# Expert biases of a top-4 mixture of experts: 64x64 tiled fp32 matmuls replaced by fp32r matmuls over the whole 128x128 array

## The chip, the core and the metric

One core of one Trainium2 chip runs the whole program. The metric is the device time of one execution in microseconds (us); the figure for a kernel is the median of its runs. Instructions run on five engines, each with its own queue in program order: PE (TensorE, matmuls; its weight loads are shown apart as PEld), DVE (VectorE), ACT (ScalarE), POOL (GpSimd) and SP (SyncE, which here issues the transfers of weights).

## The reference

A decoder block on 512 tokens of width 1024: a mixer (a state-space branch and a pooling branch), and then a mixture of 32 experts, of which each token goes to four. The change lies in the experts' biases `b_gu` and `b_down`.

```python
def moe_ffn(h, w_router, b_router, w_gu, b_gu, w_down, b_down):
    logits = xt.astype(f32) @ w_router.astype(f32) + b_router.astype(f32)
    top_val, top_idx = lax.top_k(logits, TOP_K)
    gate = jax.nn.softmax(top_val, axis=-1)
    ...
    def expert_block(args):
        xblk, e = args
        gu = xblk @ w_gu[e] + b_gu[e]              # 1024 -> 2048
        glu, lin = jnp.split(gu, 2, axis=-1)
        glu = jnp.minimum(glu, SWIGLU_LIMIT)
        lin = jnp.clip(lin, -SWIGLU_LIMIT, SWIGLU_LIMIT)
        act = glu * jax.nn.sigmoid(SWIGLU_ALPHA * glu) * (lin + 1.0)
        return act @ w_down[e] + b_down[e]         # 1024 -> 1024
    ...
    y = jax.ops.segment_sum(yb.astype(f32) * row_gate[:, None], row_tok, num_segments=T + 1)[:T]
```

## The kernel before

The mixer takes about the first 715 us; the rest is the experts. An expert's weights come as 12 pieces of 1 MB (8 for the up projection, 4 for the down projection), fetched by SP (`fetch`, L765) into a ring of buffers, as far ahead as buffers are free.

The experts are sorted by their number of tokens. An expert with more than 64 tokens is a **full block** of up to 128 rows. Its products run as three fp32r matmuls over the whole array (L1104 to L1106), for which ACT and DVE first split each half piece of weights into a high part `wh` (L113, ACT) and a low part `wl` (L114, DVE). An expert with at most 64 tokens is a **half block**: its products are fp32 matmuls with 128x64 tiles of the array (L1099), two tiles side by side; its weights need no split. A fp32 matmul leaves two records in the trace. The tiles of PSUM, `mm` and `ss`, hold one bank of 512 columns each; a half block has two column tiles in one bank, one on partitions 0 to 63 and one on 64 to 127. 17 blocks are full, 16 are half (one of these is the second block of the largest expert). The order is fixed: one full expert, two half ones, five times a full and a half one, the largest expert (a full and a half block), a half one, again five times a full and a half one, five full ones in a row, two half ones. The loop issues up(u) and then down(u-1); other small work (turning of the next rows, L1060 and L1066; gathers; activations) is hooked between the pieces.

Each bank starts with its biases: `biases` writes them into PSUM by a matmul with `start=True`, and the products add to them. The table of biases `bt` holds the 32 experts' rows as high and low parts on 64 partitions (a half of the 3072 columns on partitions 0 to 63, the other half on 64 to 127); a column with ones in two rows (`E`, from the router's tile `RM`) picks the expert. For a half block that is one 64x64 fp32 matmul per column tile (L1091): four for an up projection, two for a down projection. For a full block it is one 64x128 fp32r matmul per bank (L1093): four and two.

```python
            r, c = (n0 + n) // 3 * 64, (n0 + n) % 3 * 512
            one, rows = sel[r:r + 64, :], bt[r:r + 64, c:c + 512]
            if x.half:
                TE.matmul(rows_of(ps, n), one.bitcast(F32).to_broadcast([64, 64]), rows.bitcast(F32), start=True, stop=False)
            else:
                TE.matmul(ps[n], one.to_broadcast([64, P]), rows, start=True, stop=False)
```

POOL gathers the rows of a block from DRAM (L1046), multiplies a block's result (L1165, after ACT's L1164) and sends it to DRAM by a scatter that adds (L1168). The Tile framework's scheduler decides the order of instructions on each engine.

Of the kernel before, what the change touches and what calls it, by code (L numbers as in the profile page):

```python
# [31 lines left out]
# columns of the constant array  # L32
C_ID, C_TRI, C_IOTA, C_RC, C_P, C_P5, C_B, C_PM, C_NP = 0, 128, 256, 385, 449, 450, 451, 455, 457
C_KR, C_KC, C_BD, C_CAP, C_H = 458, 490, 491, 495, 527
C_N = 528
C_STRI, C_E = 528, 656
C_ALL = 688
# columns of the per-feature array
Q_CW, Q_CB, Q_SN, Q_PS, Q_NM, Q_C, Q_NF, Q_DS, Q_FN, Q_BA = 0, 96, 120, 136, 144, 152, 160, 168, 184, 192
Q_N = 208  # L40
# columns of the row array (one row, the same for every partition)
# [4 lines left out]
# experts in the order of the number of their tokens, after the FIXED first ones: the tokens that a rank has room for  # L46
# [18 lines left out]
def hybrid_block(ctx: ExitStack, tc: tile.TileContext, cst, cols, rows, xt, xf, wad0, wada, bada,  # L65
# [8 lines left out]
    # places that only the mixer needs stand side by side in one tile, which becomes one of the ring's  # L74
    shared = dict(t1=0, t2=512, dt=1024, ac=1152, dte=1280, eac=1408, cdk=1536, cwh=1664)
# [40 lines left out]
    # ---------------------------------------------------------------- constants  # L116
# [8 lines left out]
    ct = T_("q9", C_ALL - C_N)  # L125
    SP.dma_start(ct, cst[:, C_N:C_ALL])
    qc = T_("cols", Q_N)
    SP.dma_start(qc, cols)
# [3 lines left out]
    tri = cs[:, C_TRI:C_TRI + P]  # L132
# [27 lines left out]
    # ------------------------------------------------- activation of the conditioning  # L160
# [6 lines left out]
    # the shift and scale of the features, a quarter at a time; the first weights run between  # L167
# [22 lines left out]
    cwh = T_("cwh", 120)  # L190
    V.tensor_scalar(cwh, qc[:, 0:120], 0.5, None, op0=ALU.mult)
# [3 lines left out]
    # adaLN: groups of 512 outputs side by side, each on a quarter of the array's columns; rows, then columns  # L195
# [14 lines left out]
    # RMS statistic of x, on every partition  # L210
# [21 lines left out]
    # h of two of the eight tiles of features: the rows of the weights by their number mod 4, each on a quarter of its own  # L232
# [22 lines left out]
    # out tile of 128 features by all tokens  # L255
# [43 lines left out]
    def early():  # L299
# [6 lines left out]
        for r in range(4):  # L306
            SP.dma_start(br[r * 32:(r + 1) * 32, :], ball[:, (r // 2) * 1536:(r // 2 + 1) * 1536])
# [4 lines left out]
    # ---------------------------------------------------------------- dt  # L312
# [56 lines left out]
    # the other adaLN rows; the router's weights with the second norm's scale, and its row of constants  # L369
# [43 lines left out]
    # ---------------------------------------------------------------- pooling branch  # L413
# [15 lines left out]
    def pooled(ps, gi):  # L429
# [11 lines left out]
        tt(m[:, 0:win], s[:, 0:win], cs[:, C_RC + gi * 16:C_RC + gi * 16 + win], ALU.mult)  # L441
# [53 lines left out]
    # ---------------------------------------------------------------- SSD branch  # L495
# [78 lines left out]
    # y, features by tokens: a pair of heads side by side, each on its half of the array's columns  # L574
# [87 lines left out]
    # ---------------------------------------------------------------- gates and merge  # L662
# [51 lines left out]
    # ---------------------------------------------------------------- the adaLN rows in use from here on  # L714
# [21 lines left out]
    # weights of an expert that is known, or stands in a register  # L736
# [766 lines left out]
```

## Time and profile before

| | |
|---|---|
| median of 3 runs | 1942.31 us (1941.54 to 1943.63) |
| span of the profiled execution | 1945.2 us, no time of its own is given beside it |
| PE busy | 1867.3 us, 96% |
| PE weight loads | 1174.8 us, 60% |
| DVE busy | 1212.3 us, 62% |
| ACT busy | 947.9 us, 49% |
| POOL busy | 195.5 us, 10% |
| moved by DMA | 527.82 MB, 271 GB/s over the span |

The span runs from the first to the last instruction of one execution that the profiler recorded. Busy times are sums of instructions' times; on PE the end of a matmul overlaps the start of the next, so the distance from start to start says what a matmul costs. Times below are us from the start of the span.

### The profile page before, as it was taken

To read this page: it belongs to the slowest core of one execution; us is meant where nothing else is said; L and a number is where in the kernel's file an instruction comes from. 1 tells how busy PE (TensorE), PEld (TensorE's weight loads), DVE (VectorE), ACT (ScalarE), POOL (GpSimd) and SP (SyncE) were. 2 spreads that over 40 slices of the span, in tenths; PEclk is the share of its full clock that TensorE was granted. 3 is DMA by queue.
4 is the path that set the end of the run, shared out by engine and by line. 5 is a ranking of instruction groups with operands and counts; after the bars stand their busy time and mean duration, and the time that the engine had idled before them with its cause. 6 is when DMAs were issued, how large, how long until landed. Compare 5 with 4: busy or idle time off the path is not lost. (4 is left out here: it accounts for less than half of the span.)

```text
span 1945.2 us, 23545 instructions
## 1 busy us (share of the span) xinstructions
PE 1867.3 (96%) x8496; PEld 1174.8 (60%) x8497; DVE 1212.3 (62%) x1803; ACT 947.9 (49%) x1458; POOL 195.5 (10%) x149
## 2 busy tenths in 40 slices
PE   6999999999999999999999999999999999999995
PEld 3777687768678875545545545355464464677641
DVE  5878676746564568446646645475475474789823
ACT  4433646455452454444545544254454455677722
POOL 0000000010100000211111201022012012111111
PEclk8999999999999999999999999999999999999998
DMA  8265132343552577998999986889999999988894
GB/s 335 91 258 198 66 134 105 130 109 122 111 179 87 195 294 294 390 408 325 368 356 347 372 341 250 343 306 364 345 374 349 352 371 336 376 334 326 309 340 164
DMA packets 102441, 527.82 MB, mean 271 GB/s; under 512 B 11449, under 2 KB 11961, under 8 KB 60080
## 3 DMA queue, kind: packets, MB, share of 16 engines
q1 hardware_dynamic: 90256, 498.14, 66.6%
q0 software_dynamic: 11184, 25.50, 6.2%
q10 hardware_dynamic: 880, 2.64, 0.4%
q8 instruction: 68, 1.11, 0.2%
q14 instruction: 53, 0.43, 0.1%
HBM read 502.89 MB, written 25.77 MB: 272 GB/s over the span
## 5 line engine op out<-in xcount | busy, mean ns | idle before, releaser
L114 DVE TENSOR_TENSOR wl<-r,wh 128x1024 fp32r<-128x1024 f32 x246 | 301.9, 1251 | 125.1 <-ACT wh L113 123.7
L113 ACT ACTIVATE wh<-r 128x1024 fp32r<-128x1024 f32 x246 | 254.0, 1056 | 143.9 <-PE mm L260 56.3
L114 DVE TENSOR_TENSOR wl<-S,wh 128x1024 fp32r<-128x1024 f32 x186 | 228.5, 1262 | 41.5 <-ACT wh L113 41.0
L1105 PE MATMUL mm<-wl,S 128*128 128x512 f32 x540 | 219.4, 406 | 8.0 <-DVE wl L114 7.7
L113 ACT ACTIVATE wh<-S 128x1024 fp32r<-128x1024 f32 x186 | 189.9, 1056 | 63.7 <-PE mm L1106 37.5
L1106 PE MATMUL mm<-wh,S 128*128 128x512 f32 x540 | 216.8, 401 | 0.0
L259 PE MATMUL mm<-S,wh 128*128 128x512 f32 x512 | 207.8, 407 | 3.9 <-ACT S L113 3.9
L261 PE MATMUL mm<-S,wl 128*128 128x512 f32 x512 | 206.6, 404 | 1.5 <-DVE wl L114 1.5
L260 PE MATMUL mm<-S,wh 128*128 128x512 f32 x512 | 206.6, 404 | 0.0
L1104 PE MATMUL mm<-wh,S 128*128 128x512 f32 x540 | 179.8, 406 | 7.8 <-ACT wh L113 7.8
L1140 DVE TENSOR_SCALAR q<-mm 128x512 f32<-128x512 f32 x49 | 33.0, 688 | 162.7 <-PE mm L1099 132.1
L1165 POOL TENSOR_TENSOR y<-y,q 128x512 f32<-128x512 f32 x47 | 63.8, 1369 | 674.5 <-ACT y L1164 674.5
L1104 PEld LDWEIGHTS mm<-wh,S 128*128 128x128 f32 x540 | 101.3, 190 | 50.0 <-ACT wh L113 16.1
L1105 PEld LDWEIGHTS mm<-wl,S 128*128 128x128 f32 x540 | 103.5, 192 | 45.5 <-DVE wl L114 14.0
L1141 ACT ACTIVATE q<-q 128x512 f32<-128x512 f32 x50 | 31.3, 631 | 200.0 <-DVE q L1140 199.8
L259 PEld LDWEIGHTS mm<-S,wh 128*128 128x128 f32 x512 | 97.3, 190 | 32.8 <-issue 7.1
L1106 PEld LDWEIGHTS mm<-wh,S 128*128 128x128 f32 x540 | 103.6, 192 | 22.2
L261 PEld LDWEIGHTS mm<-S,wl 128*128 128x128 f32 x512 | 97.3, 190 | 30.9 <-issue 7.7
L260 PEld LDWEIGHTS mm<-S,wh 128*128 128x128 f32 x512 | 97.2, 190 | 26.8 <-issue 4.2
L1105 PE MATMUL ss<-wl,S 128*128 128x512 f32 x240 | 100.3, 418 | 1.0 <-DVE wl L114 0.8
L1099 PE MATMUL mm<-S,S 128*64 128x512 f32 x408 | 97.5, 597 | 0.0
L1106 PE MATMUL ss<-wh,S 128*128 128x512 f32 x240 | 96.0, 400 | 0.0
(500 smaller groups left out, 3145.7 us busy)
## 6 DMA issues: line engine op xcount, KB each, us to landing
S<-in_wgu SPq DMA_DIRECT2D x113, 1024.0 KB, 8.0
r<-in_wgu SPq DMA_DIRECT2D x97, 1024.0 KB, 8.5
S<-in_wdn SPq DMA_DIRECT2D x61, 1024.0 KB, 8.4
r<-in_wdn SPq DMA_DIRECT2D x44, 1024.0 KB, 10.9
bc<-in_wgu SPq DMA_DIRECT2D x23, 1024.0 KB, 7.5
Z<-in_wgu SPq DMA_DIRECT2D x23, 1024.0 KB, 7.7
r<-in_wada SPq DMA_DIRECT2D x16, 1024.0 KB, 6.1
r<-in_wx SPq DMA_DIRECT2D x12, 1024.0 KB, 6.2
```

Source lines behind the costliest of these rows:

```text
L113: S.activation(hi, src, AF.Copy)
L114: V.tensor_tensor(lo, src, hi.bitcast(F32), op=ALU.subtract)
L259: TE.matmul(ps, a, hh(k), start=k == 0, stop=False)
L260: TE.matmul(ps, a, hl(k), start=False, stop=False)
L261: TE.matmul(ps, b, hh(k), start=False, stop=k == KD - 1)
L1099: TE.matmul(rows_of(ps, n0 + i), x.c[k], hl[:, o + i * 512:o + (i + 1) * 512], start=False, stop=stop)
L1104: TE.matmul(p, x.h[k], h, start=False, stop=False)
L1105: TE.matmul(p, x.h[k], l, start=False, stop=False)
L1106: TE.matmul(p, x.l[k], h, start=False, stop=stop)
L1140: V.tensor_scalar(g, pg, LIM, None, op0=ALU.min)
L1141: S.activation(t, g, AF.Tanh, scale=ALPHA / 2)
L1165: G.tensor_tensor(yn, yn, gaf2[0] if half else gaf[n], op=ALU.mult)
```

## The change

The table of biases is laid out anew on the host: the even tiles of 512 columns stand on partitions 0 to 63, the odd ones on 64 to 127. A half block's two column tiles of a bank then come from one fp32r matmul over the whole array (`p` is the whole bank): the stationary operand `sel["wide"]` is a 128x128 block-diagonal matrix with the expert's column in both blocks (tiles `sw0`, `sw1`). A full block's bias is a matmul of 128 rows whose column `sel["cols"]` is zero in the other half. A new function `select`, called at the first step of the down projection before, makes these operands on POOL: one multiplication of 128x2 per expert, and two copies of 64x64 for a half block. The constants that the kernel reads at its start are split differently (two more transfers; `tri`, `rcnt` and `cwh` come into a tile that the mixer shares). Comments are removed, so line numbers shift: L1091 becomes L1097, L1093 becomes L1100, L1099 becomes L1106, L1104 to L1106 become L1111 to L1113.

```diff
@@ -304,12 +310,12 @@
         for r in range(4):
-            SP.dma_start(br[r * 32:(r + 1) * 32, :], ball[:, (r // 2) * 1536:(r // 2 + 1) * 1536])
+            SP.dma_start(br[r * 32:(r + 1) * 32, :], ball[r // 2])
         S.activation(bt, br, AF.Copy)
...
     def biases(x, ps, sel, n0):
-        for n in range(len(ps) * (2 if x.half else 1)):
-            r, c = (n0 + n) // 3 * 64, (n0 + n) % 3 * 512
-            one, rows = sel[r:r + 64, :], bt[r:r + 64, c:c + 512]
+        for n, p in enumerate(ps):
             if x.half:
-                TE.matmul(rows_of(ps, n), one.bitcast(F32).to_broadcast([64, 64]), rows.bitcast(F32), start=True, stop=False)
+                c = n0 // 2 + n
+                TE.matmul(p, sel["wide"], bt[:, c * 512:(c + 1) * 512], start=True, stop=False)
             else:
-                TE.matmul(ps[n], one.to_broadcast([64, P]), rows, start=True, stop=False)
+                h, c = (n0 + n) % 2, (n0 + n) // 2
+                TE.matmul(p, sel["cols"][:, h:h + 1].to_broadcast([P, P]), bt[:, c * 512:(c + 1) * 512], start=True, stop=False)
...
+    def sel_halves(out_, e):
+        stt(out_, cs[:, C_PM:C_PM + 2], e, cs[:, C_HM:C_HM + 2], ALU.is_equal, ALU.mult)
...
     def sel_of(u):
         if u < FIXED:
-            return sel0[:, 2 * u:2 * u + 1]
-        return rk["RM"][:, order[u]:order[u] + 1]
+            return dict(cols=sel0[:, 2 * u:2 * u + 2])
+        return dict(cols=sels[u % 2], wide=wides[u % 2])
+
+    sels = [T_(f"sel{i + 1}", 2, F32R) for i in range(2)]
+    wides = [T_(f"sw{i}", P, F32R) for i in range(2)]
+    for w in wides:
+        G.memset(w.bitcast(U32), 0)
+
+    def select(u):
+        if u >= NE:
+            return
+        both = sts[u]["half"] or u == big
+        e = rk["RM"][:, order[u]:order[u] + 1].bitcast(F32)
+        G.tensor_tensor(sels[u % 2], cs[:, C_HM:C_HM + 2], e.to_broadcast([P, 2]), op=ALU.mult)
+        for h in range(2 if both else 0):
+            hs = slice(h * 64, (h + 1) * 64)
+            G.tensor_copy(wides[u % 2][hs, hs], e[hs, :].to_broadcast([64, 64]))
...
             hooks[2] = hooks.get(2, []) + [lambda: turned(u + 1)]
+            if u >= FIXED:
+                hooks[0] = hooks.get(0, []) + [lambda: select(u + 1)]
...
+    c[:, C_HM] = i < 64
     c[:, C_H] = i >= 64
...
-        ball=A(np.concatenate([i["b_gu"][0], i["b_down"][0]], axis=1)),
+        ball=A(np.concatenate([i["b_gu"][0], i["b_down"][0]], axis=1).reshape(NE, 3, 2, 512).transpose(2, 0, 1, 3).reshape(2, NE, 1536)),
```

**PE, the up projection of a half block.** This is the place where a down projection of one half block (tile `ss_902`, products from the weights `S0`, `S1`, `S4`) ends and the banks `mm_918` and `mm_919` of the next half block's up projection are begun; in the trace of before it is the stretch from about 986 to 995 us. L1060 (L1066 after) turns rows of the next block over the whole array. Before:

```order
3443 L1060 MATMUL ss_912_6649<-cst_4_70,q10_911_6643 128x128 x4
3444 L1060 MATMUL mm_915_6663<-cst_4_70,S6_716_5259 128x128
3445 L1091 MATMUL mm_918_6697<-bt_63_381,E_698_5159 64x512
3446 L1099 MATMUL ss_902_6611<-S1_913_6656,r3_867_6297 64x512 x4
3447 L1091 MATMUL mm_918_6697<-bt_63_381,E_698_5159 64x512
3448 L1091 MATMUL mm_919_6698<-bt_63_381,E_698_5159 64x512
3449 L1099 MATMUL ss_902_6611<-S4_916_6676,r3_867_6297 64x512 x4
3450 L1091 MATMUL mm_919_6698<-bt_63_381,E_698_5159 64x512
```

After, at the same place:

```order
3443 L1066 MATMUL ss_916_6662<-cst_4_70,q10_915_6656 128x128 x4
3444 L1066 MATMUL mm_919_6676<-cst_4_70,S6_720_5267 128x128
3445 L1097 MATMUL mm_922_6710<-bt_63_383,sw0_695_5147 128x512
3446 L1097 MATMUL mm_923_6711<-bt_63_383,sw0_695_5147 128x512
3447 L1106 MATMUL ss_906_6622<-S1_917_6669,r3_871_6307 64x512 x4
```

Three stretches of 64x64 matmuls (one, two and one of them) have become two matmuls over the whole array, which stand directly behind the turning; the last four products of the down projection (`S4`) now stand further behind, after the small matmuls of the full array that follow (L1038 and others, not shown).

**PE, the down projection of a half block.** Its bank (`ss_968`, after `ss_972`) is begun among the products of a full block; in the trace of before this is at 1018 us, where a second L1091 follows at 1025 us. Before:

```order
3538 L1053 LDWEIGHTS wrt_955_6939
3539 L1053 MATMUL ss_956_6944<-GV_61_375,wrt_955_6939 128x3
3540 L1091 MATMUL ss_968_7094<-bt_63_381,E_698_5159 64x512
3541 L1105 MATMUL ss_934_6781<-wl0_710_5229,S7_901_6610 128x512
3542 L1106 MATMUL ss_934_6781<-wh0_708_5227,S7_901_6610 128x512
```

After:

```order
3537 L1059 LDWEIGHTS wrt_959_6951
3538 L1059 MATMUL ss_960_6956<-GV_61_377,wrt_959_6951 128x3
3539 L1097 MATMUL ss_972_7106<-bt_63_383,sw0_695_5147 128x512
3540 L1112 MATMUL ss_938_6792<-wl0_714_5237,S7_905_6621 128x512
3541 L1113 MATMUL ss_938_6792<-wh0_712_5235,S7_905_6621 128x512
```

The place of the first of the two is kept; the second one is gone.

**POOL, the making of the selectors.** A stretch of POOL's queue after the change, one full and one half expert long, with what each instruction waits for in brackets; L1052 gathers rows, L1172 multiplies a result, L1175 sends it. Before, the same queue holds these three kinds alone.

```order
58 L1052 DMA S6_720_5267<-h_d_4671,idx_1_896_6484 80x1024 [waits DVE_49,PE_49]
59 L1276 CAST sw0_695_5147<-E_702_5167 64x64 [waits PE_49]
60 L1276 CAST sw0_695_5147<-E_702_5167 64x64 [waits DMASW2_49,DMASW3_49,DMASW1_49,Pool_49]
61 L1172 TENSOR_TENSOR y_887_6424<-y_887_6424,q8_580_4361 128x512 [waits Activation_49,Pool_49]
62 L1172 TENSOR_TENSOR y_887_6424<-y_887_6424,q9_581_4362 128x512 [waits Activation_49]
63 L1175 DMA y_d_124<-y_887_6424,idx_3_757_5565 640x1024 [waits Pool_49]
64 L1273 TENSOR_TENSOR sel2_694_5146<-cst_4_70,E_702_5167 128x2 [waits PE_49]
65 L1052 DMA S6_720_5267<-h_d_4671,idx_2_928_6738 128x512 [waits DVE_49]
```

The two copies of a half expert's selector stand between a gather and a multiplication, and the second one waits for gathers and scatters on POOL's DMA queue; the multiplication for a full expert's selector stands behind a scatter.

## Rows read from the trace of the kernel before

**Rows 1.** The page's busy time, share of the span and instructions of each engine.

```profile
PE 1867.3 (96%) x8496; PEld 1174.8 (60%) x8497; DVE 1212.3 (62%) x1803; ACT 947.9 (49%) x1458; POOL 195.5 (10%) x149
```

**Rows 2.** Busy time by stretch (from:to, length, then busy us and instructions of PE, PEld, DVE, ACT, POOL, then granted clock of PE as a share of the full one, busy share of the DMA engines, GB/s): nearly the whole expert phase, and one period of a full and a half expert.

```profile
720.00:1900.00 1180.00, 1146.49 (x5000) 641.90 (x5001) 723.36 (x1001) 606.08 (x851) 170.50 (x115) 0.99 0.92 345
955.90:1028.60 72.70, 70.08 (x308) 38.38 (x307) 42.40 (x57) 36.12 (x52) 10.01 (x7) 1.00 0.94 360
```

**Rows 3.** Waits in the expert phase, from 720 us on: who waited for what, us in total, how often, the longest. SPq is the queue that fetches the weights, L765 its issue.

```profile
SPq L765 <- DVE wl L114: 436.5, 163, 7.9
SPq L765 <- PE ss L1099: 215.9, 62, 5.5
ACT wh L113 <- DMA S<-in_wgu: 13.7, 2, 12.2
```

**Rows 4.** The matmuls that write biases, grouped by line, operands and shape: count, then busy us and mean ns of one, then idle time before them and what ended it.

```profile
L1091 PE MATMUL mm<-bt,E 64*64 64x512 f32 x120 | 43.0, 612 | 0.0
L1091 PE MATMUL ss<-bt,E 64*64 64x512 f32 x72 | 31.9, 627 | 0.0
L1093 PE MATMUL mm<-bt,E 64*128 64x512 f32 x64 | 29.4, 484 | 5.4 <-DVE q L1142 4.5 <-ACT q L1068 0.4 <-ACT b L1068 0.4
L1093 PE MATMUL ss<-bt,E 64*128 64x512 f32 x32 | 12.4, 452 | 0.0
```

**Rows 5.** PE in order of time (start, duration, instruction, how many in the row), where a half block's up projection is begun.

```profile
987.89 0.27 PE L1060 MATMUL mm<-cst,S 128*128 128x128 f32 x1
988.09 1.07 PE L1091 MATMUL mm<-bt,E 64*64 64x512 f32 x2
989.09 1.94 PE L1099 MATMUL ss<-S,r 128*64 128x512 f32 x8
990.96 1.08 PE L1091 MATMUL mm<-bt,E 64*64 64x512 f32 x4
991.97 1.94 PE L1099 MATMUL ss<-r,r 128*64 128x512 f32 x8
993.83 1.07 PE L1091 MATMUL mm<-bt,E 64*64 64x512 f32 x2
994.83 0.18 PE L1032 MATMUL ss<-tokc,a 128*128 128x2 bf16 x1
```

**Rows 6.** The same view, where a half block's down projection is begun among a full block's products.

```profile
1018.22 0.25 PE L1053 MATMUL ss<-GV,wrt 128*128 128x3 bf16 x4
1018.41 1.07 PE L1091 MATMUL ss<-bt,E 64*64 64x512 f32 x2
1019.41 0.50 PE L1105 MATMUL ss<-wl,S 128*128 128x512 f32 x1
1019.74 0.39 PE L1106 MATMUL ss<-wh,S 128*128 128x512 f32 x1
1019.97 0.39 PE L1105 MATMUL ss<-wl,S 128*128 128x512 f32 x1
...
1024.59 0.62 PE L1104 MATMUL ss<-wh,S 128*128 128x512 f32 x2
1025.15 1.07 PE L1091 MATMUL ss<-bt,E 64*64 64x512 f32 x2
1026.14 0.51 PE L1105 MATMUL ss<-wl,S 128*128 128x512 f32 x1
1026.49 0.40 PE L1106 MATMUL ss<-wh,S 128*128 128x512 f32 x1
```

**Rows 7.** The same view, where a full block's up projection is begun among a half block's products, and the end of these; in brackets the idle time before a row and what ended it.

```profile
998.80 0.50 PE L1093 MATMUL mm<-bt,E 64*128 64x512 f32 x1
999.23 1.94 PE L1099 MATMUL mm<-r,S 128*64 128x512 f32 x8
...
1012.02 0.50 PE L1093 MATMUL mm<-bt,E 64*128 64x512 f32 x1
1012.88 0.49 PE L1093 MATMUL mm<-bt,E 64*128 64x512 f32 x1 [0.36 <-DVE q L1142]
1014.21 0.55 PE L1060 MATMUL ss<-cst,q 128*128 128x128 f32 x3 [0.84 <-DVE q L107]
```

**Rows 8.** Busy time by stretch, columns as in rows 2: a full block's up projection, its down projection (in which the next half block's down projection is begun), the next full block's up projection, and a full block's down projection in the row of five full ones.

```profile
955.90:979.50 23.60, 22.17 (x94) 16.87 (x92) 18.74 (x16) 16.05 (x17) 4.68 (x3) 1.00 0.99 382
1012.00:1028.60 16.60, 15.40 (x73) 10.50 (x72) 13.58 (x20) 10.32 (x12) 1.35 (x1) 1.00 1.01 401
1028.60:1053.70 25.10, 23.67 (x93) 18.08 (x91) 18.89 (x16) 16.05 (x17) 4.67 (x3) 0.93 1.00 386
1709.20:1726.50 17.30, 16.96 (x81) 11.70 (x79) 17.30 (x21) 15.10 (x25) 0.00 (x0) 1.00 0.71 262
```

**Rows 9.** POOL in order of time around one gather (first two rows); the transfers from 990 to 1110 us, by kind, with the median us from issue to landing (third row); and PE where the next half block's up projection is begun (last row).

```profile
1017.71 1.35 POOL L1046 DMA_INDIRECT S<-h_d,idx  x1 [17.69 <-issue]
1029.14 2.52 POOL L1165 TENSOR_TENSOR y<-y,q 128x512 f32<-128x512 f32 x2 [10.09 <-ACT y L1164]
S<-h_d,idx POOLq DMA_INDIRECT x4, 6.0
1062.35 1.07 PE L1091 MATMUL mm<-bt,E 64*64 64x512 f32 x2
```

**Rows 10.** What the DMA engines moved from 990 to 1110 us, GB/s in 40 slices of 3 us.

```profile
GB/s 284 355 318 173 324 420 416 429 421 431 414 315 414 419 283 329 347 422 429 431 415 410 117 328 213 281 354 264 249 337 412 429 429 437 426 412 412 422 419 212
```

More of the change, by code (lines that the diff above doesn't have):

```diff
@@ L30 @@
 ALPHA = 1.702
[L33 to L40, printed above, removed]
+C_ID, C_IOTA, C_P, C_P5, C_B, C_PM, C_NP = 0, 128, 257, 258, 259, 263, 265
+C_KR, C_KC, C_BD, C_CAP, C_HM = 266, 298, 299, 303, 335
+C_H, C_N = C_HM + 1, C_HM + 2
+C_TRI, C_RC = C_N, C_N + 128
+C_STRI = C_RC + 64
+C_E = C_STRI + 128
+C_ALL = C_E + 32
+Q_CB, Q_CW = 96, 120
+Q_SN, Q_PS, Q_NM, Q_C, Q_NF, Q_DS, Q_FN, Q_BA = 0, 16, 24, 32, 40, 48, 64, 72
+Q_N = 88
 R_AL, R_DB, R_BR = 0, 32, 64
@@ L72, in hybrid_block @@
     uid = [0]
-    shared = dict(t1=0, t2=512, dt=1024, ac=1152, dte=1280, eac=1408, cdk=1536, cwh=1664)
+    shared = dict(t1=0, t2=512, dt=1024, ac=1152, dte=1280, eac=1408, cdk=1536, cwh=1664, tri=1784)
     Z = sb.tile([P, 2048], F32, tag="Z", name="Z")
@@ L124, in hybrid_block @@
     SP.dma_start(cs, cst[:, 0:C_N])
-    ct = T_("q9", C_ALL - C_N)
-    SP.dma_start(ct, cst[:, C_N:C_ALL])
+    ct = T_("q9", C_ALL - C_STRI)
+    SP.dma_start(ct, cst[:, C_STRI:C_ALL])
     qc = T_("cols", Q_N)
-    SP.dma_start(qc, cols)
+    SP.dma_start(qc, cols[:, Q_CW:Q_CW + Q_N])
+    cwh, trc = T_("cwh", Q_CW), T_("tri", C_STRI - C_TRI)
+    SP.dma_start(cwh, cols[:, 0:Q_CW])
+    SP.dma_start(trc, cst[:, C_TRI:C_STRI])
     rw = T_("rows", R_N)
@@ L131, in hybrid_block @@
     ident = cs[:, C_ID:C_ID + P]
-    tri = cs[:, C_TRI:C_TRI + P]
+    tri, rcnt = trc[:, 0:P], trc[:, P:P + 64]
     iota = cs[:, C_IOTA:C_IOTA + P]
@@ L189, in hybrid_block @@
     V.tensor_tensor(b12[32:64, :], b12r[32:64, :], b12[32:64, :].bitcast(F32), op=ALU.subtract)
-    cwh = T_("cwh", 120)
-    V.tensor_scalar(cwh, qc[:, 0:120], 0.5, None, op0=ALU.mult)
+    V.tensor_scalar(cwh, cwh, 0.5, None, op0=ALU.mult)
     y_d = dr.tile([T + P, D], F32, name="y_d")
@@ L440, in pooled @@
         stt(m[:, win:512], s[:, win:512], 1.0 / win, u[:, win:512], ALU.mult, ALU.subtract)
-        tt(m[:, 0:win], s[:, 0:win], cs[:, C_RC + gi * 16:C_RC + gi * 16 + win], ALU.mult)
+        tt(m[:, 0:win], s[:, 0:win], rcnt[:, gi * 16:gi * 16 + win], ALU.mult)
         tt(m[:, 0:win], m[:, 0:win], u[:, 0:win], ALU.subtract)
@@ L1231, in tabled @@
         eT = T_("eT", 2, F32R)
-        V.tensor_scalar(eT, cs[:, C_PM:C_PM + 2], ec[:, 0:1], None, op0=ALU.is_equal)
-        return dict(pos=lambda b: pu[:, b:b + 1], gv=lambda b: gvu[:, b * 3:(b + 1) * 3], sel=eT[:, 0:1], **weights(ev))
+        sel_halves(eT, ec[:, 0:1])
+        return dict(pos=lambda b: pu[:, b:b + 1], gv=lambda b: gvu[:, b * 3:(b + 1) * 3], sel=dict(cols=eT), **weights(ev))
     def pos_of(u):
@@ L1318, in rows_from_here @@
         xe2.extend([xet[:, 0:D], xet[:, D:2 * D]])
-    extra = {0: {0: [rows_from_here, permute], 1: [lambda: prep(1)], 2: [gates], 3: [permute_gates], 4: [lambda: prep(0)],
+    extra = {0: {0: [rows_from_here, permute], 1: [lambda: prep(1), lambda: select(1)], 2: [gates], 3: [permute_gates], 4: [lambda: prep(0)],
                  6: [first_gates, lambda: prep(2)]},
```

2 lines of the change are left out of this document (1 added, 1 removed).

## The prediction

> **What bounds the kernel now.** I read first the busy times of the page, then those by stretch, then the waits, then PE in order of time. PE is busy for 96% of the span, no other engine for more than 62% [rows 1]. In the expert phase it is busy 1146.49 of 1180.00 us, 97%, at 0.99 of its full clock (the 2.4 GHz level) [rows 2]. The reader should then rule out the transfers: their engines are 0.92 busy over the same stretch [rows 2], which looks like a second bound. The queue that fetches weights waits, however, for buffers to come free (436.5 us for DVE's low parts, 215.9 us for PE's products), while an engine waits for weights only twice, 13.7 us in all [rows 3]. So the weights run ahead and PE sets the pace; what leaves PE's queue leaves the span, except where PE would then wait for the splits of ACT and DVE.
>
> **The biases of half blocks.** 192 records are removed, 43.0 + 31.9 = 74.9 us busy [rows 4]. Busy times overlap on PE: a stretch is drawn as 1.07 us, yet the next instruction starts after 1.00 (988.09 to 989.09, and 1018.41 to 1019.41) [rows 5, 6]. So they occupy about 74.9 x 1.00 / 1.07 = 70 us. One matmul of a column tile (2 records) and two of them on both halves (4 records) take the same, 1.00 and 1.01 us [rows 5]: where one stands alone, the place of the second one goes unused. A regular half expert has five such stretches, three in its up and two in its down projection, 5.0 us.
>
> In their place come three matmuls per half expert, 16 x 3 = 48. The trace holds no fp32r matmul of this operand, but the products L1105 and L1106 have the same shape (128x128 by 512 columns), and a new one starts every 0.23 us (1019.74 to 1019.97) [rows 6]. I take 0.23, since all but the contents of the operand is the same: 48 x 0.23 = 11 us. The upper bound is the mean of a bias matmul of a full block today, 0.484 us busy [rows 4]; by it the 48 cost 23 us, 12 more. Saved: 70 - 11 = 59 us.
>
> The stretches also delay their neighbours. In the full block's products, the L1105 behind a stretch takes 0.33 and 0.35 us to the next start instead of 0.23, and two L1104 ahead of one take 0.56 (1024.59 to 1025.15) instead of 2 x 0.23 [rows 6]. That is 0.2 us per stretch, and after the change the matmul in that place has the shape of its neighbours. With two stretches for each of 16 blocks it is 6.5 us; I take 4, since the blocks at both ends of the order stand elsewhere. In the up projection nothing of this is saved, since the products L1099 on both sides stay tiled. The Trainium skill, TensorEngine Tiling (Array Packing), Key Properties, says that changing the tiling mode drains TensorE. The 0.10 to 0.12 us on either side of a stretch in rows 6 agree; by the rule taken for every stretch the sum would be the 6.5 us, by my choice of rows it is 4. The same page's table of theoretical speedups speaks against the change: with at most 64 rows of contraction, tiles should be up to 2x faster than the whole array. The pair at 1.01 us in rows 5 shows that two tiles do run at once, but the array's fp32r price of 0.23 us lies below even half of that; by the rule alone the new form would have to lose, by the rows it gains.
>
> **The biases of full blocks.** Their number stays at 102, 96 of which are in rows 4. A 64-row one between half products takes 0.43 us (998.80 to 999.23) [rows 7]; with 128 rows, next to other full-array matmuls, it is worth 0.23. Of the two at the end of a half block nothing is gained: PE waits for DVE there anyway, 0.36 and 0.84 us [rows 7]. I count 0.3 us for each of the ten or so regular periods, 3 us. In the five full blocks in a row DVE is busy for all 17.30 us of the down projection [rows 8], so nothing is gained there. Bounds: 0, and 102 x 0.2 = 20 us if every one gained; nearer to the low one, since most stand in full-array products or in waits.
>
> **What is lost again.** In the full block's down projection, in which the half block's down biases lie, DVE is busy 13.58 of 16.60 us [rows 8]. There the change takes out 2 x 1.00 + 0.4 - 0.23 = 2.2 us, which leaves 14.4 us, and DVE would be 94% busy; ACT with 10.32 has room. A small part of the saving will turn into waits for the low parts: I take 0.3 us in each of ten periods, 3 us. Bounds: nothing, and all of it, 2.2 x 11 = 24 us.
>
> **The selectors, the start.** POOL's work is costed at nothing. The second copy of a wide selector waits for the gather ahead of it in the queue: issued at 1017.71, 1.35 us on POOL, 6.0 us to land, so it is there at 1025.1 us. The multiplication queued behind it waits for ACT until 1029.14 anyway, and PE wants the selector for the next half block only at 1062.35 [rows 9]: 37 us of cover. POOL is 10% busy [rows 1]. If the cover were gone, each us late would cost PE one us in each of 15 half experts. The two more transfers at the start and the changed small DVE operations lie beside the loads of the mixer; I give them 0, with a bound of 1 us either way.
>
> **The sum.** 59 + 4 + 3 - 3 = 63 us, about 4.7 us per regular period of 72.7 us. The profiled execution spans 1945.2 us, 2.9 above the median of 1942.31; its span would become 1882, and the median **1879 us**.
>
> **The rivals.**
> 1. *The full block's down projection becomes bound by DVE.* For it speaks the 94%, against it that DVE splits ahead of PE and that 13.58 still lies below 14.4. All of the 24 us would be lost instead of 3: 1900 us. Chance 0.10.
> 2. *The clock falls more often.* One full up projection took 25.10 us at a granted 0.93, another 23.60 at 1.00 [rows 8]; the first holds a wait of PE for splits near its start. If every one of eleven up projections fell to it, 1.5 x 11 = 16 us would go if none fell now; since about half may do so already, it is 8 us in either direction: 1887 us. Chance 0.08, and as much the other way, to 1871.
> 3. *The wide matmul costs 0.48 us,* the upper bound: 12 us more, 1891 us. Chance 0.07.
> 4. *The transfers become the bound.* A period moves 360 GB/s x 72.7 us = 26.2 MB at a busy share of 0.94 [rows 2]; at a share of one and the same efficiency, 383 GB/s, it takes 68.4 us, against the 68.0 that the sum leaves. That costs 0.4 x 11 = 4 us, 1883 us, and lies within the forecast's range. Whole slices at 410 to 437 GB/s [rows 10] say that there is more room, a floor near 62 us. Chance 0.07.
> 5. *Slower: the selector comes late.* Should its copy miss the turn in front of the multiplication and come only after the next half block wants it, PE stands still. The point from which it decides is 37 us of delay for any loss, and 41 us (63 / 15 = 4.2 more) for a slower kernel. At 44 us it would be 7 x 15 - 63 = 42 us slower, 1984 us. Against it speaks the 6.0 us landing [rows 9]. Chance 0.03.
> 6. *Nothing changes,* because PE then waits for weights or splits wherever it is ahead: 1942 us. The waits of rows 3 exclude it nearly. Chance 0.02.
>
> The forecast itself has 0.55 (1872 to 1887), with 0.08 for the clock's gain.
>
> **How the numbers follow.** The low end: 6.5 instead of 4 for the neighbours, no loss to DVE, and the clock's 8 us, 1879 - 13.5 = 1865. The high end takes in rivals 1, 2 and 3 one at a time: 1900. Outside lie rivals 5 and 6 and combinations of the first three, some 0.1 to 0.15. A difference under 0.2% (4 us) can hardly be told from none by a measurement of this kernel. Faster is everything but rivals 5 and 6: 0.95; same 0.02; slower 0.03.
>
> **What would show it.** In the changed kernel's trace: the 48 matmuls of L1097 start to start 0.23 us, about 11 us in all where 70 were; the L1112 behind one no longer longer than its neighbours; a regular period near 68 us; waits of PE for low parts in the full block's down projection up by 0.3 us a period, not 2; the second copy on POOL done near the gather's landing, some 35 us before PE's use; PE still 95% busy or more, and the fetches still waiting for buffers. The prediction would be wrong if L1097 took twice as long, if PE's waits for splits grew by more than 20 us in all, or if PE waited for POOL.

## The result and the profile after

The changed kernel takes 1871.53 us (median of four runs, 1868.54 to 1873.43) against 1942.96 us before: 0.9634 of it, 95% interval 0.9614 to 0.9654, 71 us less. A second set of five runs gave 1873.1 us and 0.965 (0.9625 to 0.9676). Forecast were 1879 us, 63 us less, between 1865 and 1900. The profiled execution spans 1869.1 us.

Busy times of the changed kernel from the page, and the stretches that answer to [rows 2] and [rows 8]: nearly the whole expert phase, one period of a full and a half expert, and its last part, the full block's down projection, cut as in [rows 8].

```profile
PE 1788.1 (96%) x8353; PEld 1165.1 (62%) x8353; DVE 1213.9 (65%) x1803; ACT 947.0 (51%) x1458; POOL 220.0 (12%) x214
```

```profile
715.50:1850.00 1134.50, 1093.36 (x4956) 640.31 (x4958) 731.10 (x1010) 608.28 (x854) 190.75 (x165) 1.00 0.95 363
934.60:1002.50 67.90, 65.15 (x298) 37.93 (x297) 42.23 (x57) 36.05 (x52) 10.59 (x10) 1.00 0.98 381
987.90:1002.50 14.60, 13.40 (x69) 10.29 (x68) 13.57 (x20) 10.30 (x12) 1.68 (x3) 1.00 1.02 393
```

A period at the full clock takes 67.9 us instead of 72.7 [rows 2]: 4.8 us less, where the sum had 4.7. PE lost 79 us of busy time and is still the bound. The full block's down projection takes 14.6 us instead of 16.6; the sum had 14.4. DVE is busy for 13.57 us of it, 93%, and PE idles for 1.2 us, as long as before: these are the two waits for `q` of [rows 7], 0.36 and 0.83 us here. No wait for low parts has come up in this period.

The matmuls of half blocks, grouped by line (answers to [rows 4]; both kinds of bank):

```profile
L1097 PE MATMUL mm<-bt,sw 128*128 128x512 f32 x30 | 11.3, 441 | 0.0
L1097 PE MATMUL ss<-bt,sw 128*128 128x512 f32 x18 | 8.6, 478 | 0.0
```

PE in order of time, where a half block's up projection is begun (answers to [rows 5]), where a matmul over the whole array stands behind small bf16 ones, and where a half block's down projection is begun (answers to [rows 6]):

```profile
966.70 0.27 PE L1066 MATMUL mm<-cst,S 128*128 128x128 f32 x1
966.72 0.71 PE L1097 MATMUL mm<-bt,sw 128*128 128x512 f32 x2
967.37 1.94 PE L1106 MATMUL ss<-S,r 128*64 128x512 f32 x8
...
991.27 0.48 PE L1112 MATMUL ss<-wl,S 128*128 128x512 f32 x1
991.59 0.39 PE L1113 MATMUL ss<-wh,S 128*128 128x512 f32 x1
...
994.15 0.25 PE L1059 MATMUL ss<-GV,wrt 128*128 128x3 bf16 x4
994.26 0.48 PE L1097 MATMUL ss<-bt,sw 128*128 128x512 f32 x1
994.58 0.39 PE L1112 MATMUL ss<-wl,S 128*128 128x512 f32 x1
994.81 0.40 PE L1113 MATMUL ss<-wh,S 128*128 128x512 f32 x1
```

Two wide matmuls take 0.65 us to the next start (966.72 to 967.37), one takes 0.32 (994.26 to 994.58), and the L1112 behind it has its ordinary 0.23.

**Two parts of the gain.** Each run lists the mean granted clock of PE, and the time of one execution goes with it: a straight line through all 123 runs of this study, with a level of its own for each kernel and one common slope, has 1.6 us for each 0.001 of the clock and leaves a scatter of 1.4 us. The level below is that line's value at a clock of 0.988, so kernels can be compared apart from what the clock did. From four runs a level is known to about 1.5 us, and the difference of two levels to about 2 us (95%).

| kernel | median us | ratio to before, 95% | mean clock (runs) | level at 0.988, us |
|---|---|---|---|---|
| before | 1942.96 | 1 | 0.9855 (59) | 1937.8 |
| before, again | 1941.89 | 1.0002, 0.9984 to 1.002 | in the row above | |
| constants alone | 1943.16 | 1.0003, 0.999 to 1.0016 | 0.9844 (12) | 1936.8 |
| full blocks alone | 1934.53 | 0.9951, 0.9933 to 0.997 | 0.9881 (10) | 1933.0 |
| wide in fp32 | 1900.35 | 0.9789, 0.9768 to 0.9809 | 0.9885 (4) | 1902.3 |
| wide in fp32, up only | 1887.68 | 0.972, 0.9701 to 0.9739 | 0.9910 (4) | 1893.5 |
| wide in fp32, down only | 1872.97 | 0.9643, 0.9623 to 0.9663 | 0.9915 (4) | 1878.3 |
| half blocks alone | 1876.37 | 0.9664, 0.9639 to 0.9689 | 0.9880 (4) | 1876.5 |
| wide matmul twice | 1886.6 | 0.9717, 0.9696 to 0.9737 | 0.9898 (4) | 1889.0 |
| **changed** | 1871.53 | 0.9634, 0.9614 to 0.9654 | 0.9889 (9, both sets) | 1873.5 |
| selectors on ACT | 1873.68 | 0.9642, 0.9623 to 0.9661 | 0.9900 (5) | 1876.4 |
| sending later | 1856.25 | 0.9558, 0.9537 to 0.9579 | 0.9908 (4) | 1859.8 |
| both of these | 1859.06 | 0.9573, 0.9551 to 0.9595 | 0.9910 (4) | 1864.3 |

At an equal clock the change gives 1937.8 - 1873.5 = 64.3 us, against the 63 of the sum. The mean clock rose from 0.9855 to 0.9889, which is worth 3.4 x 1.6 = 5 to 6 us more. The traces say the same: in stretches of 2 us I counted 11 falls of the granted clock in the profiled execution of before (one at its start and one at its end among them, as in every trace), 32.9 us of full speed lost, and 7 in that of after, 20.3 us lost. The spans differ by 76.1 us, 12.6 of them from this, and 63.5 are left; 1 to 2 us of these lie in the mixer and are chance (see the constants alone). (The profiled execution of before lies above its median, so its share of the clock is larger than in the mean of the runs.)

### The profile page after: what moved, and what is told of

The parts are those of the page before. It is cut to its first block, busy times and chain, and to the rows that moved or that the text cites. A ratio compares the mean times of both kernels' runs of the same rounds, so it can differ in the third digit from the quotient of the medians.

```text
span 1869.1 us, 23339 instructions
## 1 busy us (share of the span) xinstructions
PE 1788.1 (96%) x8353; PEld 1165.1 (62%) x8353; DVE 1213.9 (65%) x1803; ACT 947.0 (51%) x1458; POOL 220.0 (12%) x214
## 5 line engine op out<-in xcount | busy, mean ns | idle before, releaser
L1112 PE MATMUL mm<-wl,S 128*128 128x512 f32 x540 | 217.3, 402 | 9.7 <-DVE wl L118 9.0
L1113 PE MATMUL mm<-wh,S 128*128 128x512 f32 x540 | 214.5, 397 | 0.0
L1111 PE MATMUL mm<-wh,S 128*128 128x512 f32 x540 | 177.7, 402 | 8.0 <-ACT wh L117 8.0
L1147 DVE TENSOR_SCALAR q<-mm 128x512 f32<-128x512 f32 x49 | 32.9, 687 | 181.8 <-PE mm L1106 153.1
L1112 PEld LDWEIGHTS mm<-wl,S 128*128 128x128 f32 x540 | 102.2, 189 | 47.6 <-DVE wl L118 17.0
L1111 PEld LDWEIGHTS mm<-wh,S 128*128 128x128 f32 x540 | 100.6, 188 | 48.7 <-ACT wh L117 16.3
L1113 PEld LDWEIGHTS mm<-wh,S 128*128 128x128 f32 x540 | 102.4, 190 | 21.5
L1112 PE MATMUL ss<-wl,S 128*128 128x512 f32 x240 | 97.1, 405 | 1.9 <-DVE wl L118 1.5
L1106 PE MATMUL mm<-S,S 128*64 128x512 f32 x408 | 96.2, 596 | 0.0
L1172 POOL TENSOR_TENSOR y<-y,q 128x512 f32<-128x512 f32 x47 | 67.7, 1453 | 237.9 <-ACT y L1171 237.2
L1113 PE MATMUL ss<-wh,S 128*128 128x512 f32 x240 | 95.5, 398 | 0.0
```

The source lines that it names most:

```text
L1106: TE.matmul(rows_of(ps, n0 + i), x.c[k], hl[:, o + i * 512:o + (i + 1) * 512], start=False, stop=stop)
L1111: TE.matmul(p, x.h[k], h, start=False, stop=False)
L1112: TE.matmul(p, x.h[k], l, start=False, stop=False)
L1113: TE.matmul(p, x.l[k], h, start=False, stop=stop)
L1147: V.tensor_scalar(g, pg, LIM, None, op0=ALU.min)
L1172: G.tensor_tensor(yn, yn, gaf2[0] if half else gaf[n], op=ALU.mult)
```

## The experiments

Each kernel is the changed one with the edit shown, unless it says otherwise.

**Half blocks alone.** Full blocks contract over 64 rows again.

```diff
-                TE.matmul(p, sel["cols"][:, h:h + 1].to_broadcast([P, P]), bt[:, c * 512:(c + 1) * 512], start=True, stop=False)
+                TE.matmul(p, sel["cols"][h:h + 64, h // 64:h // 64 + 1].to_broadcast([64, P]), bt[h:h + 64, c * 512:(c + 1) * 512], start=True, stop=False)
```

(here `h` is 0 or 64.)

> The changed kernel with the biases of full blocks as before: 64 rows of contraction, a 64x128 tile, in the new layout of the table (the half blocks keep the matmul over the whole array). My theory: the full blocks' part is worth about 3 us (0.3 in each of ten regular periods), so this takes 1871.5 + 3 = 1874 to 1875 us. Rival: every one of the 102 gains 0.2 us, then it takes about 1892 us. If the full blocks' part is worth nothing, 1871 to 1872 us.

Measured: 1876.37 us, 0.3% above the changed kernel, 3.0 us by the levels. The full blocks' part is about as large as forecast, within the error of 2 us, but not where I put it: in the row of five full blocks a period takes 40.2 us in the changed kernel, 40.7 here and 40.6 before, while a regular period takes 68.0 us here (937.41 to 1005.41) against 67.9, so 0.1 us and not the 0.3 of the forecast.

**Full blocks alone.** Half blocks write each column tile by a 64x64 fp32 matmul again.

```diff
-                TE.matmul(p, sel["wide"], bt[:, c * 512:(c + 1) * 512], start=True, stop=False)
+                for h in (0, 64):
+                    TE.matmul(p[h:h + 64, :], sel["wide"][h:h + 64, h:h + 64].bitcast(F32), bt[h:h + 64, c * 512:(c + 1) * 512].bitcast(F32), start=True, stop=False)
```

> The changed kernel with the biases of half blocks as before: fp32 matmuls of 64x64 tiles, four for an up and two for a down projection, here in the new layout of the table; they stand alone or in pairs at the same places as before the change. Full blocks, selectors on POOL and the start are as changed. My theory: nearly the whole gain is theirs, so this takes about 1943 - 3 (full blocks) - 2 (start) = 1938 us. Rival: the clock or the start gave more than I think, then it is 1930 us or less. If POOL's work costs something that the gain hides, it is above 1943 us.

Measured: 1934.53 us, 4.8 us below before by the levels; that the median lies 3 us under the 1938 expected goes with a mean clock of 0.9881 instead of 0.9855. Against the changed kernel the half blocks' part is 1933.0 - 1873.5 = 59.5 us; by half blocks alone it is 1937.8 - 1876.5 = 61.3. POOL's selectors are in this kernel too, so they cost no more than the full blocks gain.

**Wide matmul in fp32.** Three stretches per half block remain, in the old type.

```diff
-                TE.matmul(p, sel["wide"], bt[:, c * 512:(c + 1) * 512], start=True, stop=False)
+                TE.matmul(p, sel["wide"].bitcast(F32), bt[:, c * 512:(c + 1) * 512].bitcast(F32), start=True, stop=False)
```

> The changed kernel with the 48 wide matmuls of half blocks in fp32 instead of fp32r; shape, number and selectors are kept. This parts the gain in two: fewer stretches (three instead of five per half block), and the cheaper type. My theory: a fp32 matmul of 512 columns takes 1.00 us in any tile, so this is slower than the changed kernel by 48 x 0.77 = 37 us, 1908 us, and 35 us faster than before. Rival: most of the gain comes from no longer switching the tiling of the array and from the missing stretches; then it loses under 20 us, 1890 us or less.

Measured: 1900.35 us; by the levels 28.8 us above the changed kernel, between the theory's 37 and the rival's 20, and 30.7 below the kernel with full blocks alone. PE in this kernel, where a half block's up projection is begun:

```profile
906.81 1.02 PE L1097 MATMUL mm<-bt,sw 128*128 128x512 f32 x2
907.76 1.94 PE L1106 MATMUL ss<-S,r 128*64 128x512 f32 x8
909.63 1.13 PE L1097 MATMUL mm<-bt,sw 128*128 128x512 f32 x2
910.68 1.94 PE L1106 MATMUL ss<-S,r 128*64 128x512 f32 x8
```

One wide fp32 matmul (two records) takes 0.95 and 1.05 us, as much as a 64x64 one in [rows 5]. So the 59.5 us have two halves of nearly the same size: fewer stretches (one matmul for two column tiles) and the cheaper type. In a regular period at the full clock the first is 2.5 us (72.6 us in the kernel with full blocks alone, 70.1 here), of which two stretches' own time is 2.0; the second is 2.2 us (67.9 in the changed kernel). Neither is mainly a matter of switching.

**Wide matmul twice.** A second matmul adds the same to the bank, so the biases of half blocks count twice.

```diff
                 TE.matmul(p, sel["wide"], bt[:, c * 512:(c + 1) * 512], start=True, stop=False)
+                TE.matmul(p, sel["wide"], bt[:, c * 512:(c + 1) * 512], start=False, stop=False)
```

> The changed kernel with each of the 48 wide matmuls issued twice, the second one added (half blocks get their biases twice, which is left so). It prices one wide matmul. My theory: 0.23 us each, 11 us, 1882 to 1883 us. Rival, the upper bound of the prediction: 0.48 us each, 1894 us. If PE has slack there, less than 6 us.

Measured: 1886.6 us, 15.5 us above the changed kernel by the levels, 0.32 us for each of the 48, more than the theory's 0.23. The reason is in PE's rows of this kernel (L1098 is the added line):

```profile
902.27 0.48 PE L1097 MATMUL mm<-bt,sw 128*128 128x512 f32 x1
902.59 0.40 PE L1098 MATMUL mm<-bt,sw 128*128 128x512 f32 x1
902.91 1.94 PE L1107 MATMUL ss<-S,r 128*64 128x512 f32 x8
904.78 0.50 PE L1097 MATMUL mm<-bt,sw 128*128 128x512 f32 x1
905.12 0.40 PE L1098 MATMUL mm<-bt,sw 128*128 128x512 f32 x1
905.36 0.18 PE L1038 MATMUL ss<-tokc,a 128*128 128x2 bf16 x1
```

Beside tiled products the first of a pair takes 0.32 to 0.34 us and the second 0.32 ahead of tiled products, 0.24 ahead of full-array ones. 0.23 us is the price among equal neighbours alone. The scheduler also put the second bank's pair behind a group of products here, so part of the 15.5 us is a switch that the changed kernel has not.

**Wide matmul in fp32 for one projection.** Two kernels: the one shown, and one with `not n0` as the condition (`n0` is 0 for the up projection, 4 for the down projection).

```diff
-                TE.matmul(p, sel["wide"], bt[:, c * 512:(c + 1) * 512], start=True, stop=False)
+                wd, bc = sel["wide"], bt[:, c * 512:(c + 1) * 512]
+                if n0:
+                    wd, bc = wd.bitcast(F32), bc.bitcast(F32)
+                TE.matmul(p, wd, bc, start=True, stop=False)
```

> The changed kernel with the wide matmul of half blocks in fp32 for the down projection only (16 of 48). In nine regular up projections of full experts PE waits 1.4 us near the head; the granted clock fell there in 21 of 45 in the traces of the five kernels so far with fp32 biases (the kernel before twice, its constants alone, full blocks alone, wide fp32), and in 5 of 45 in the five with fp32r (changed twice, half blocks alone, wide twice, selectors on ACT), though the wait is the same. Theory: the fp32 bias in the full block's down projection, some 7 to 13 us ahead of the head, decides; then 3 to 5 of nine fall here, and the time is 16 x 0.6 = 10 us above the changed kernel at an equal clock. Rival: the place does not matter or all is chance; then 0 to 2 fall.

> The other part: fp32 for the up projection's wide matmuls only (32 of 48), fp32r for the down projection's. Theory: 0 to 2 of the nine heads fall, as in the changed kernel, and the time is 32 x 0.65 = 21 us above it at an equal clock. Rival: 3 or more fall, then the place of the fp32 matmuls does not decide.

Measured: 1872.97 us for the down projections alone, 1887.68 us for the up projections alone, 4.8 and 20.0 us above the changed kernel by the levels; together 24.8, the kernel with all in fp32 has 28.8. The 20.0 are about as expected (21), the 4.8 half of the 10 expected: in the traces a regular down projection, from its first product to the next up projection, takes 12.7 us instead of 12.1, the expected 0.6, but only about ten of the 16 lie in such a place. Two of nine heads fell in either trace, fewer than the theory's 3 to 5 for the down projections, so its type is not shown to decide; nine heads are few. What decides where the clock falls stays open (below).

**The constants alone.** The kernel before with the new layout of the constants: `biases`, the table, `sel_of` and the hooks of before; the diff is that of the change without them.

> The kernel before with only the constants laid out as in the change (two more transfers at the start, three arrays in a shared tile); biases, their table and their selectors are those of before, no work on POOL. In the trace of the changed kernel the mixer's instructions run 1.65 us earlier from 30 us on, and 6 us earlier from 525 us on, behind a place where the kernel before waits 3.8 us for DVE at a granted clock of 0.84. My theory: the 1.65 us are the new layout's, the rest is an accident of the profiled execution: 1 to 2 us faster than before. Rival: the layout removes the mixer's wait too, then 4 to 6 us faster and a mean granted clock of 0.988 instead of 0.985. No effect: within 1 us.

Measured: 1943.16 us, ratio 1.0003 (0.999 to 1.0016): no effect. The mixer's earlier end in the trace of after (715.5 instead of 721.6 us) was an accident of the two profiled executions: with the new layout alone it ends at 714.2, in the second trace of before, without it, at 716.3 us.

**Selectors on ACT.**

```diff
-        G.tensor_tensor(sels[u % 2], cs[:, C_HM:C_HM + 2], e.to_broadcast([P, 2]), op=ALU.mult)
+        S.activation(sels[u % 2], cs[:, C_HM:C_HM + 2], AF.Copy, scale=e)
...
-            G.tensor_copy(wides[u % 2][hs, hs], e[hs, :].to_broadcast([64, 64]))
+            S.activation(wides[u % 2][hs, hs], e[hs, :].to_broadcast([64, 64]), AF.Copy)
```

> The changed kernel with the selectors made by ACT instead of POOL, at the same step. In the changed kernel's trace POOL's second copy waits for the gather ahead of it; in some full up projections (at 1073.9 us for one) POOL's multiplication behind it then falls on DVE's splits, which run 1.7 us for one instead of 1.2, and the stage takes 24.5 us instead of 23.7. My theory: that is what POOL's part of the change costs, so this is 2 to 4 us faster than the changed kernel. Rival: ACT's extra instructions delay its own splits by as much: within 1 us, or slower.

Measured: 1873.68 us, 2.9 us above the changed kernel by the levels. The effect on POOL is there and is given back. First POOL, DVE and PE of the changed kernel around one gather, in order of time:

```profile
1071.99 0.40 POOL L1276 CAST sw<-E 64x64 fp32r<-64x64 f32 x1 [4.12 <-DMA S<-h_d,idx]
1073.88 3.52 POOL L1172 TENSOR_TENSOR y<-y,q 128x512 f32<-128x512 f32 x2
1076.17 3.45 DVE L118 TENSOR_TENSOR wl<-S,wh 128x1024 fp32r<-128x1024 f32 x2
1078.54 0.50 PE L1112 MATMUL mm<-wl,S 128*128 128x512 f32 x1 [0.81 <-DVE wl L118]
```

Two splits take 3.45 us there instead of 2.35. Then the busy times of this up projection in the changed kernel, of its counterpart with the selectors on ACT, and a wait of PE in a down projection of the latter:

```profile
1072.30:1096.80 24.50, 22.49 (x94) 16.84 (x92) 19.58 (x16) 16.09 (x17) 6.83 (x5) 1.00 1.03 405
```

```profile
1074.20:1097.80 23.60, 22.12 (x94) 16.82 (x92) 18.76 (x16) 16.03 (x17) 4.71 (x3) 1.00 1.02 404
```

```profile
1000.22 0.51 PE L1112 MATMUL ss<-wl,S 128*128 128x512 f32 x1 [0.15 <-DVE wl L118]
```

The up projection is 0.9 us shorter. Summed over the trace, the full blocks' up projections take 2 to 3 us less than in the second trace of the changed kernel, but their down projections some 3.7 us more: there ACT's copies stand ahead of its splits, and PE waits for low parts. That is a loss of about 1 us; the rest of the 2.9 lies within the error.

**Sending later.** ACT's scalings of a full block's result move behind the first piece of the next up projection.

```diff
-                send(psd[0], sts[v])
+                if v < NE - 2 and not sts[v]["half"] and len(psd) == 1:
+                    pend.append(lambda p=psd[0], st=sts[v]: send(p, st))
+                else:
+                    send(psd[0], sts[v])
```

> The changed kernel with the scaling and sending of a full block's result moved from the end of its down projection to the second piece of the next up projection, so that ACT's two scalings stand behind two splits more. At the head of each up projection of a full expert PE waits 1.4 to 1.5 us for splits behind these scalings, and in a part of them the granted clock falls to its 1.2 GHz level for 3.4 us, which costs 1.5 us more. Theory: the wait is ACT's queue order and the fall follows the wait: 11 x 1.4 + about 3 x 1.5 = 20 us faster than the changed kernel, 1852 us, with a mean granted clock of 0.991 or more. Rival: the wait moves to the next split or to DVE, less than 6 us.

Measured: 1856.25 us, 15 us less than the changed kernel, 13.7 by the levels. The head of a full up projection, first in the changed kernel, then here:

```profile
1004.56 0.73 PE L1111 MATMUL mm<-wh,S 128*128 128x512 f32 x2 [0.52 <-ACT wh L117]
1005.50 0.50 PE L1111 MATMUL mm<-wh,S 128*128 128x512 f32 x1 [0.21 <-ACT wh L117]
1006.80 0.79 PE L1112 MATMUL mm<-wl,S 128*128 128x512 f32 x1 [0.79 <-DVE wl L118]
```

```profile
998.17 1.09 PE L1111 MATMUL mm<-wh,S 128*128 128x512 f32 x4
999.74 0.50 PE L1112 MATMUL mm<-wl,S 128*128 128x512 f32 x1 [0.48 <-DVE wl L118]
```

1.5 us of waits have become 0.5 (at most 1.3 at the other heads), and the stage takes 22.3 us instead of 23.7 to 23.8 at the full clock. The 0.73 us of waits for ACT's high parts are gone, so they were ACT's queue order. The 0.79 us for DVE's low part are not ACT's alone: the split that PE waits for takes 2.20 us instead of 1.2 beside POOL's multiplication (the rows at 1003.13 and 1004.54 at the end of this document). Here the multiplication still meets the splits, and 0.48 us of the wait remain:

```profile
997.46 3.36 DVE L118 TENSOR_TENSOR wl<-Z,wh 128x1024 fp32r<-128x1024 f32 x2 [1.66 <-ACT wh L117]
```

These two splits take 3.36 us instead of 2.35. What POOL alone costs at the heads no run parts from ACT's order. The gain could be had beside the change: this is the fastest kernel of the study, 0.9558 of before, though 13.7 us of the 20 expected.

**Both.**

> Both: selectors made by ACT, and a full block's result scaled and sent one piece later. Theory: the two effects add, 2 to 4 us below the kernel with the later sending alone. Rival: with the sending moved, POOL's multiplication no longer meets the same splits, and ACT's selectors bring nothing or cost 1 to 3 us.

Measured: 1859.06 us, 4.5 us above the later sending alone by the levels: the rival holds, ACT's selectors bring nothing and cost a little.

**Both kernels once more.**

> The changed kernel once more, unaltered, for the granted clock. Over the runs so far the time of one execution goes with its mean granted clock, about 1.6 us for each 0.001; the kernel before has a mean of 0.9855 over 30 runs, the changed one 0.9892 over four. Theory: the change itself gives some 64 us at an equal clock (1873 against 1938 us at 0.988), and the rest of the 71 us, about 6, comes from a higher mean clock that will show again: mean clock 0.989, 1870 to 1873 us, and 7 falls of the clock (to its 1.2 GHz level) in the trace, give or take 2. Rival: the four runs had luck: mean clock 0.986 to 0.987 and 1875 to 1877 us.

Measured: 1873.1 us; the mean clock of all nine runs is 0.9889, as the theory had it; 5 falls in the second trace.

> The kernel before once more, unaltered, for a second trace: its first one holds 11 falls of the clock, two of them in the mixer, five at the head of a full expert's up projection. Theory: about as many again, 9 to 13, most of the five at other heads than in the first trace. Rival: 6 to 7 as in the changed kernel, so that the first trace was an accident.

Measured: 12 falls in the second trace, four at the heads of regular full up projections. The higher clock of the changed kernel is no accident of one profile.

**What stays open.** The fall at a head looks alike in both kernels. Here it is in steps of 3 us, before and after the change:

```profile
1028.60:1031.60 3.00, 2.29 (x10) 1.24 (x8) 0.99 (x1) 3.00 (x5) 2.45 (x2) 1.00 1.03 423
1031.60:1034.60 3.00, 2.28 (x6) 1.65 (x7) 3.00 (x3) 1.82 (x2) 2.21 (x2) 0.76 0.91 300
1034.60:1037.60 3.00, 3.00 (x11) 2.36 (x10) 2.69 (x3) 1.91 (x2) 0.00 (x0) 0.67 1.00 329
```

```profile
1002.50:1005.50 3.00, 2.27 (x9) 1.24 (x7) 0.96 (x1) 3.00 (x5) 2.60 (x3) 1.00 1.00 407
1005.50:1008.50 3.00, 2.20 (x5) 1.60 (x6) 3.00 (x3) 1.84 (x2) 2.33 (x2) 0.71 1.02 407
1008.50:1011.50 3.00, 3.00 (x11) 2.35 (x11) 2.78 (x3) 1.85 (x2) 0.00 (x0) 0.73 1.04 407
1011.50:1014.50 3.00, 3.00 (x15) 2.46 (x14) 2.45 (x2) 1.90 (x3) 0.00 (x0) 1.00 1.03 306
```

PE waits for splits in the first two stretches, then the clock is at its 1.2 GHz level for part of the second and third. Of nine such heads per trace, 21 of 45 fell in the five traces with all half biases in fp32, 5 of 45 in the five with fp32r, 4 of 18 in the two mixed ones, and none of 18 with the later sending, which takes away most of the wait. The falls come right behind the wait. That taking the wait away prevents them is not shown: at 5 in 45, two of 18 heads would fall. Nor is it shown why the wait leads to a fall less often after the change. (At the last of the nine heads PE waits 0.7 us instead of some 1.5 in the kernels whose selectors POOL makes, so the wait is not quite the same everywhere.)

## Why the prediction was right, point by point

- **The bound.** PE stayed at 96%, the fetches still wait mostly for buffers, and the four rivals that would have eaten the gain (DVE, transfers, POOL, nothing) did not come. The transfers' busy share rose to 0.98 in a period at 381 GB/s, near the 383 that rival 4 took for the limit; the splits still hardly wait for weights.
- **Half blocks: 59 + 4 us forecast, less 3 for waits; 59.5 measured** (full blocks alone against the changed kernel, by the levels). Inside the term two errors met. The price of a wide matmul was taken as 0.23 us, from equal neighbours [rows 6]; in its place it costs 0.32 us behind small bf16 matmuls or ahead of tiled products. 48 x 0.32 = 15 us instead of 11. The 3 us of new waits did not come where the sum put them, in the regular periods, though DVE's share there, 93%, is what it said (94%). Over the whole trace PE's waits for low parts in down projections rose all the same, from 1.0 to 3.3 us (3.6 in the second trace). All of it stands in the row of five full blocks and behind it, where the sum had nothing; one such wait before and after:

```profile
1718.92 0.50 PE L1105 MATMUL ss<-wl,S 128*128 128x512 f32 x1 [0.22 <-DVE wl L114]
1653.50 0.50 PE L1112 MATMUL ss<-wl,S 128*128 128x512 f32 x1 [0.76 <-DVE wl L118]
```

  In the kernel with full blocks alone this wait is 0.77 us (1713.01), in the one with half blocks alone 0.22 (1659.58): in the row it comes from the full blocks. Three waits of 0.3 us behind the row (1766 to 1774) stand in half blocks alone too and not in full blocks alone. That the size of this term was nearly right is luck.
- **The neighbours' 0.2 us per stretch.** Right for the second stretch of a down projection, which is gone. At the first one the 0.10 us behind it only moved into the wide matmul (0.32). The same 0.32 stands at 991.27, where an L1112 follows bf16 matmuls of the same 128x128 tile, so such a delay needs no change of the tile. What the tile has in it can be read from fp32 over the whole array, first in the kernel with fp32 for the down projection alone, then, ahead of such a matmul, in the one with all in fp32:

```profile
994.48 1.10 PE L1100 MATMUL ss<-bt,sw 128*128 128x512 f32 x2
995.02 0.79 PE L1115 MATMUL ss<-wl,S 128*128 128x512 f32 x1
995.65 0.39 PE L1116 MATMUL ss<-wh,S 128*128 128x512 f32 x1
```

```profile
774.32 0.39 PE L1113 MATMUL ss<-wh,S 128*128 128x512 f32 x1
774.56 1.88 PE L1097 MATMUL mm<-bt,sw 128*128 128x512 f32 x4
```

  The bias and the product behind it take 1.17 us (994.48 to 995.65) against 1.33 in 64x64 tiles (1018.41 to 1019.74, [rows 6]): 0.16 less at an unchanged type. Ahead of a fp32 matmul over the whole array a product keeps its 0.24 us (774.32 to 774.56), where [rows 6] had 0.56 for two, 0.10 more than usual. So some of the delay does go with the tile. The rule of the Trainium skill, TensorEngine Tiling (Array Packing), Key Properties, that a switch of the mode drains TensorE, agrees with these, but not with the 0.32 at 991.27. The table of speedups in the Trainium skill, TensorEngine Tiling (Array Packing), Theoretical Speedup, did not decide: fp32 in 64x64 tiles and fp32 over the whole array take about the same 1 us, and fp32r a third of it in place.
- **Full blocks: 3 us forecast, 3.0 measured** against the changed kernel, 4.8 against the kernel before, each to about 2 us. I had given the row of five full blocks 0 because DVE is busy throughout its down projection [rows 8], and 0.3 to each regular period, which gained 0.1. That stage went from 17.30 us to 16.60 with DVE still busy all the time; the up projection behind it gave 0.3 back, and the new 0.54 us of waiting for low parts (above) stand in the stage, so DVE does bind there in part. A stage cut by PE's marks is still not bound by the engine that fills it, since DVE's own period has slack in the up projection. Below is this stage in the changed kernel.

```profile
1643.90:1660.50 16.60, 15.63 (x80) 11.77 (x79) 16.60 (x21) 14.40 (x24) 0.00 (x0) 1.00 0.73 255
```

- **POOL and the start at nothing.** The start: right (1.0003). POOL: the cover was as forecast. In the changed kernel the second copy ends behind the gather, and PE wants it 33 us later:

```profile
993.61 1.33 POOL L1052 DMA_INDIRECT S<-h_d,idx  x1 [16.83 <-DVE idx L1048]
1002.50 0.24 POOL L1276 CAST sw<-E 64x64 fp32r<-64x64 f32 x1 [7.20 <-DMA S<-h_d,idx]
1036.12 0.71 PE L1097 MATMUL mm<-bt,sw 128*128 128x512 f32 x2
```

  What I had not costed is the instruction behind it: where the gather lands late, POOL's multiplication moves onto DVE's splits. In the first trace it is 0.4 to 0.8 us in three regular up projections, and 1.0 in that of the largest expert, 2 to 3 us.
- **The clock.** Rival 2 gave it 8 us in either direction, and 1871 us for the better one. That side came true in part, with 5 to 6 us; it is nearly the whole distance between 1879 and 1871.5. At the heads, where rival 2 put it, four or five of nine fell in the two traces before, one and none in those after: about four at some 1.5 us each. That fewer would fall had no reason in the prediction, only a chance of 0.08, and the cause is open; the change itself gave 64 us against 63.

## What to carry to other kernels

Price a new instruction by a row that has its neighbours too: among equal ones a fp32r matmul of 512 columns costs 0.23 us, beside others 0.32. When two causes come in one edit (fewer instructions, a cheaper type), a kernel that has only one of them parts the gain at once. Read the granted clock of every run before crediting a change with its last 0.3%: here 1.6 us went with each 0.001.

## What the runs showed of the hardware

- Among tiled products a fp32 matmul of 512 columns takes about 1.0 us to the next start whether it fills a 64x64 tile (1.00) or the whole array (0.95 and 1.05). Two 64x64 ones that stand together take 1.01 us [rows 5], so they run at once; a lone one takes 1.00.
- DVE's split and POOL's multiplication get in each other's way: a split that begins while POOL multiplies takes 2.20 us (1004.54, below) instead of 1.2, and ends 1.1 us after POOL does. It was so before the change too: 2.14 us at 1030.61. The Trainium skill, SBUF — State Buffer, section on the two separate sides, says that DVE with two inputs in SBUF, and GpSimd where it reads SBUF, take a shared pair of ports by an exclusive lock for a whole instruction. These rows agree: POOL ends at 1005.66, DVE at 1006.74.

```profile
1003.13 2.53 POOL L1172 TENSOR_TENSOR y<-y,q 128x512 f32<-128x512 f32 x2 [0.40 <-ACT y L1171]
1004.54 2.20 DVE L118 TENSOR_TENSOR wl<-r,wh 128x1024 fp32r<-128x1024 f32 x1 [2.80 <-ACT wh L117]
```
